# Rows of softmax sums stored from GpSimd's queue and gates stored from ScalarE's queue, both formerly from SyncE's, in a two-layer encoder

## The chip, the cores and the metric

The kernel runs on one core of a Trainium2 chip. The metric is the device time of one execution in microseconds (us), taken as the median of several runs. The engines are named as the profile names them: PE is TensorE (matmuls), DVE is VectorE, ACT is ScalarE, POOL is GpSimd, SP is SyncE, which here does nothing but issue DMAs. An issue of a DMA from ACT or SP stands in the profile as ACTq or SPq.

## The reference

A trunk of two encoder layers runs over two groups of tokens, 512 ("sample") and 256 ("prompt"), width 1024. Each layer normalises its input, modulates it by a condition, projects it, and feeds three mixers: A, dense latent attention with 8 heads; B, dilated windows with 3 x 4 heads, combined by their softmax denominators; C, 2-D neighbourhood attention with 8 heads. Each mixer is gated, projected, merged by sigmoid gates, and put through one output projection with a residual.

```python
def encoder_layer(...):
    h = rmsnorm(x, g_pre) * (1 + scale) + shift
    z = h @ w_in
    o_a = mla_attention(...)            # softmax over all tokens
    o_b = dilated_attention(...)        # softmax over three windows together
    o_c = neighbourhood_attention(...)  # softmax over 8 x 16 neighbours
    p_a = (o_a * silu(gate_a)) @ w_pa   # p_b and p_c likewise
    mg = sigmoid(merge)                 # three gates of width 1024
    out = (mg[0] * p_a + mg[1] * p_b + mg[2] * p_c) @ w_out
    return x + gate * rmsnorm(out, g_post)
```

## The kernel before, in words

Features lie on the 128 partitions and the 768 tokens of both groups side by side, 0 to 511 the sample's and 512 to 767 the prompt's. Every fp32 operand of a matmul is split into a high and a low part: ACT casts the high part, DVE or POOL subtracts (`sub_lo`, line 160), and PE runs three products. Weights come through a ring of three raw buffers (`load_split`, line 165), are split by ACT at line 177 and by `sub_lo`, and are multiplied in `feat_mm` (line 201).

For each layer the stages are `branch_a`, `branch_b`, `branch_c`, `merge`, `project`. In A and C the scores go key by key: keys on the partitions, queries along the row. A softmax (`soft_keys`, line 658) so needs a maximum and a sum across partitions. DVE first combines the key tiles (lines 662 and 664), POOL then reduces across the partitions (line 665) and leaves the result on all of them. The steps are: maximum, subtraction on DVE (line 670), exponential on ACT (line 671), sum. The exponentials are split again and multiplied with the values in `pv` (ACT line 679, DVE line 680, PE line 683; the result is o_ps); they are not divided by the sum there. Instead one row of each sum is sent to a DRAM table, `den_scr` (line 672; in B line 869). Once a pair of heads is complete, `row_gains` (line 686) reads its sums back in another shape (line 689), takes reciprocals on DVE (line 690), writes those (line 691) and reads them spread over the partitions (line 695). DVE multiplies the pair's outputs with them (line 655; in C line 1012), and `finish_pair` sends them to DRAM (line 446) for `merge`, which loads them again (line 1046).

The small tiles of a softmax (the combined maximum, the reduced maximum, the combined sum, the reduced sum) are slots of a ring of six, `S`. The stored row lies in such a slot, so the slot is free only when the store has read it.

To keep PE busy during the softmaxes, `early` (line 1021) multiplies gates of the merge stage ahead of time. ACT writes tanh of such a gate into a tile `the` (line 1019; one buffer), and a DMA takes it to `th_scr` in DRAM (line 1027). The table `FILL` says how many gates go where. In `merge` the gates come back (line 1051).

POOL runs reductions, some of the low parts (every second or third, by the table `LO_POOL`), additions and memsets. Between reductions and plain tensor operations the program has an operation without operands (`ISA` in the order of instructions), by which POOL changes from one kind to the other.

A scheduler sets the order of instructions on each engine. It follows the dependences and its own model of durations, and the engine that issues a DMA is part of what it plans with; an edit of one issue can so move instructions everywhere. Each engine, and each engine's DMA issues, runs in order: what stands behind a waiting instruction waits with it.

The lines that the change touches are 672, 869 and 1027. Lines named below have the same numbers in both kernels.

Of the kernel before, what the change touches and what calls it, by code (L numbers as in the profile page):

```python
# [16 lines left out]
ALU = mybir.AluOpType  # L17
# [49 lines left out]
def trunk_kernel(ctx, tc, x_t, c_row, c_col, w_ada0, w_ada, cols, w_a, w_feat, w_val, w_val2, w_uqk, w_qr, w_uv, w_pj, w_o,  # L67
                 bias_s, bias_p, rope_t, rope_k, mask_b, mask_c, y_t):
    nc = tc.nc
# [18 lines left out]
    def U(tag, dt=F32, name=None):  # L88
        return pool.tile([P, T], dt, tag=tag, name=name or tag, bufs=BUFS[tag])
# [51 lines left out]
    th_scr = dram.tile([depth, 24, P, T], F32, name="th_scr")  # L141
    row_scr = dram.tile([depth, 28, P], F32, name="row_scr")
    den_scr = dram.tile([depth, 10, 2, 1, T], F32, name="den_scr")
# [241 lines left out]
    def halves(t):  # L385
        return t[:, :256], t[:, 256:]
# [92 lines left out]
    def latents(l, h, hl):  # L479
# [87 lines left out]
        while pend:  # L567
            flip(*pend.pop(0))
        early(l, h, min(LATE_E, FILL[l][0]))
        do_jobs(gates, GATES[l][-1], c_)  # L570
        ada_gain(l)
        pend = [(j, (3, 4, 5)) for j in range(6)]
        early(l, h, FILL[l][0] - LATE_E, lambda k, mm: flips(mm))
        while pend:
            flip(*pend.pop(0))
        return cn, krs

    def branch_a(l, h_, h):
# [13 lines left out]
        va = None  # L592
        for pr in range(4):
            early(l, h, FILL[l][1 + 2 * pr])
            if pr % 2 == 0:

# [34 lines left out]
            for e in range(2):  # L631
                hd = (pr % 2) * 2 + e
                (qs, qrs), ka = qn[e], kn[e]
                prods = ((ka, qs), (kb[e], qs), (krs, qrs))
                tq = [U("tq") for _ in range(4)]
                for g, (o, n) in enumerate(GROUPS):
                    nk = n // P

                    for k0 in range(0, nk, 1 + g):
                        sp = SP()  # L640
                        for k in range(1 + g):
                            kc = slice(o + (k0 + k) * P, o + (k0 + k + 1) * P)
                            for j, (w, a) in enumerate(prods):
                                nc.tensor.matmul(sp[:, k * 256:k * 256 + n], w[:, kc], a[:, o:o + n],
                                                 start=(j == 0), stop=(j == 2))
                        for k in range(1 + g):
                            nc.scalar.copy(tq[k0 + k][:, o:o + n], sp[:, k * 256:k * 256 + n])  # L647
                for g, (o, n) in enumerate(GROUPS):
                    xs = [x[:, o:o + n] for x in tq[:n // P]]
                    soft_keys(xs, n, den_scr[l, pr, e, 0:1, o:o + n])  # L650
                    o_ps = ps_o.tile([P, NS], F32, tag="o", name="o_ps")[:, :n]
                    for k, x in enumerate(xs):
                        pv(x, [(o_ps, vslice(va, hd, o // P + k), lambda a: a)], k == 0, k == n // P - 1)
                    out_half(o_ps, o_t, e, [(lambda a: a[:, o:o + n], lambda a: a)])
# [3 lines left out]
    def soft_keys(xs, n, den):  # L658

        def across(op):  # L660
            out, red = (S(), S()) if n > 256 else halves(S())
            nc.vector.tensor_tensor(out, xs[0], xs[1], op=op)  # L662
            for x in xs[2:]:
                nc.vector.tensor_tensor(out, out, x, op=op)
            nc.gpsimd.partition_all_reduce(red, out, P, RED.max if op == ALU.max else RED.add)  # L665
            return red

        m = across(ALU.max)
        for x in xs:
            nc.vector.tensor_sub(x, x, m)  # L670
            nc.scalar.activation(x, x, AF.Exp)  # L671
        nc.sync.dma_start(out=den, in_=across(ALU.add)[0:1])

    def pv(x, terms, first, last):

# [112 lines left out]
    def branch_b(l, h, hl):  # L788
# [4 lines left out]
        for hd in range(4):  # L793
            e = hd % 2
# [38 lines left out]
            for g, (o, n) in enumerate(GROUPS):  # L833
# [32 lines left out]
                across(sm, ALU.add)  # L866
                dn = S()
                nc.gpsimd.partition_all_reduce(dn[:, :n], sm[:, :n], P, RED.add)  # L868
                nc.sync.dma_start(out=den_scr[l, 4 + hd // 2, e, 0:1, o:o + n], in_=dn[0:1, :n])

                o_ps = ps_o.tile([P, NS], F32, tag="o", name="o_ps")
                ov = o_ps[:, :n].rearrange("p (s i) -> p s i", s=SB[g])
# [75 lines left out]
    def branch_c(l, h, hl):  # L948
        state["phase"] = "c"
        vcs = None  # L950
        for pr in range(4):
# [12 lines left out]
            for e in range(2):  # L964
# [30 lines left out]
                for g, (o, n) in enumerate(GROUPS):  # L995
                    xs = [x[:, o:o + n] for x in tq]
                    soft_keys(xs, n, den_scr[l, 6 + pr, e, 0:1, o:o + n])
                    o_ps = ps_o.tile([P, NS], F32, tag="o", name="o_ps")
                    v = lambda k: vslice(vc, hd % 4, k)
                    if g == 0:  # L1000
                        lo_, hi_, mid = (lambda a: a[:, 0:256]), (lambda a: a[:, 256:512]), (lambda a: a[:, 128:384])
                        pv(xs[0], [(c(o_ps), v(k), c) for k, c in ((0, lo_), (2, hi_))], True, False)
                        pv(xs[1], [(c(o_ps), v(k), c) for k, c in ((1, mid), (3, ends))], False, True)
                    else:
                        for k in range(2):
                            pv(xs[k], [(o_ps[:, :256], v(4 + k), lambda a: a)], k == 0, k == 1)
                    out_half(o_ps, o_t, e, natural(g))
# [8 lines left out]
    def merge_gate(l, idx, h, th, between=None):  # L1016
        mg = feat_mm(w_feat[l, F_MG + idx], KT, h, name="mg", between=between)
        for g, (o_, n) in enumerate(GROUPS):
            nc.scalar.activation(th[:, o_:o_ + n], mg[g], AF.Tanh, scale=0.5)  # L1019

    def early(l, h, n, between=None):

        for _ in range(n):
            idx = 23 - len(ahead)
            th = U("f", name="the")
            merge_gate(l, idx, h, th, between)
            nc.sync.dma_start(out=th_scr[l, idx], in_=th)
            ahead.add(idx)

    def do_jobs(jobs, n, cact):  # L1030
# [170 lines left out]
    for t_ in range(T // P):  # L1201
        x, x2 = U("cv", name="x"), x2s[t_ // 3][:, t_ % 3 * 256:t_ % 3 * 256 + 256]
        nc.sync.dma_start(out=x, in_=x_t[t_, :, :T])
        if t_ % 3 == 0:
            nc.sync.dma_start(out=x2s[t_ // 3].rearrange("p (t c) -> p t c", c=256),
                              in_=x_t[t_:t_ + 3, :, T:].rearrange("t p c -> p t c"))
# [22 lines left out]
    for t_, pieces in enumerate(xs):  # L1229
        for i, x in enumerate(pieces):  # L1230
            e = (NORM0, NORM1)[i][t_]
# [6 lines left out]
    for l in range(depth):  # L1238
        hl = act_list(h)
        ahead.clear()  # L1240
        branch_a(l, h, hl)
        branch_b(l, h, hl)
        branch_c(l, h, hl)
        mixed = merge(l, hl)
        h = project(l, mixed, l == depth - 1)
# [166 lines left out]
```

## Time and profile before

| what | us |
|---|---|
| median of 3 runs | 1964.03 (1962.99 to 1964.36) |
| the profiled execution | 1966.35 |
| its span, from the first instruction to the last | 1964.6 |
| PE busy | 1845.0 (94%) |
| DVE busy | 1530.9 (78%) |
| ACT busy | 1018.6 (52%) |
| POOL busy | 664.2 (34%) |

The time of the profiled execution is that of one run, 2.3 us above the median; the span is what the trace covers. Busy times overlap between engines. A busy PE isn't PE at its peak, since matmuls are pipelined and the clock that is granted to PE varies between two levels, 1.2 and 2.4 GHz; the profile gives it as a share of the higher one for any stretch.

### The profile page before, as it was taken

What the parts mean: (1) busy time and instruction counts of PE and PEld (TensorE: products, weight loads), DVE (VectorE), ACT (ScalarE), POOL (GpSimd) and SP (SyncE); (2) the same over time, 40 slices, a digit from 0 to 9 for tenths busy, and PEclk for the clock granted to TensorE, in tenths of its full rate; (3) what the DMA queues carried; (4) which work ended last, traced back from release to release, by engine and by line L of the source; (5) the groups of instructions that cost most, each with busy time, mean ns of one, the idle gap of its engine ahead of it and who ended that gap; (6) DMA issues with size and microseconds to landing.
All of it is one profiled execution on the core that took longest, in us unless ns stands there. A gap on an engine that the chain in (4) does not pass through costs nothing. (4 is left out here: it accounts for less than half of the span.)

```text
span 1964.6 us, 30204 instructions
## 1 busy us (share of the span) xinstructions
PE 1845.0 (94%) x10674; PEld 1638.1 (83%) x10674; DVE 1530.9 (78%) x3018; ACT 1018.6 (52%) x2123; POOL 664.2 (34%) x432
## 2 busy tenths in 40 slices
PE   7897999999989987999999999999999999987998
PEld 6886888888877876888999888889888778876898
DVE  8957768579987999896587467687699868997763
ACT  5356556356577455322464356574566684653241
POOL 6404415202221454316534024253022212454570
PEclk9998999999999999999999999999999999998999
DMA  8432241232313233445452332422222222233652
GB/s 294 150 117 62 86 139 57 71 99 82 92 54 92 79 117 115 167 143 191 140 197 89 124 99 88 135 76 86 87 85 85 88 75 89 87 107 99 217 174 71
DMA packets 94904, 221.25 MB, mean 113 GB/s; under 512 B 18096, under 2 KB 32504, under 8 KB 94752
## 3 DMA queue, kind: packets, MB, share of 16 engines
q1 hardware_dynamic: 90144, 213.02, 33.4%
q10 hardware_dynamic: 4608, 6.29, 1.1%
q8 instruction: 84, 1.38, 0.3%
q14 instruction: 68, 0.56, 0.1%
HBM read 173.78 MB, written 28.18 MB: 103 GB/s over the span
## 5 line engine op out<-in xcount | busy, mean ns | idle before, releaser
L665 POOL PARTITION_ALL_REDUCE fixed<-fixed x128 | 314.2, 2486 | 496.3 <-DVE fixed L662 337.0
L201 PE MATMUL mg<-fixed 128*128 128x512 f32 (+1 forms) x2304 | 436.2, 342 | 1.4 <-DVE o_t L397 0.7
L201 PEld LDWEIGHTS mg<-fixed 128*128 128x128 f32 x2304 | 360.3, 191 | 51.6 <-PE sp L984 1.0
L177 ACT CAST fixed<-fixed 128x512 fp32r<-128x512 f32 (+1 forms) x332 | 199.5, 606 | 339.3 <-PE mg L201 117.8
L160 DVE TENSOR_TENSOR fixed<-fixed,fixed 128x512 fp32r<-128x512 f32 (+3 forms) x309 | 224.2, 729 | 113.9 <-ACT fixed L177 110.7
L201 PE MATMUL qkb<-fixed 128*128 128x512 f32 (+1 forms) x1152 | 211.9, 338 | 0.0
L201 PEld LDWEIGHTS qkb<-fixed 128*128 128x128 f32 x1152 | 177.0, 189 | 24.2
L201 PE MATMUL gate<-fixed 128*128 128x512 f32 (+1 forms) x960 | 184.0, 341 | 1.6 <-DVE tq L830 1.3
L201 PEld LDWEIGHTS gate<-fixed 128*128 128x128 f32 x960 | 150.0, 191 | 22.0 <-DVE tq L830 1.5
L1064 PE MATMUL pp<-hi,fixed 128*128 128x512 f32 (+1 forms) x640 | 161.5, 340 | 5.0 <-ACT th L1019 4.7
L680 DVE TENSOR_TENSOR fixed<-tq,fixed 128x512 fp32r<-128x512 f32 (+1 forms) x160 | 127.9, 821 | 2.7 <-ACT fixed L679 2.5
L1064 PEld LDWEIGHTS pp<-hi,fixed 128*128 128x128 f32 x640 | 111.9, 192 | 19.9 <-ACT th L1019 5.1
L671 ACT ACTIVATE tq<-tq 128x512 f32<-128x512 f32 (+1 forms) x160 | 83.4, 545 | 82.7 <-DVE tq L670 82.5
L429 POOL MEMSET kb<- 64x768 f32 x56 | 41.1, 736 | 209.5 <-PE sp L820 121.0
L670 DVE TENSOR_TENSOR tq<-tq,fixed 128x512 f32<-128x512 f32 (+1 forms) x160 | 97.8, 660 | 16.3 <-POOL fixed L665 16.2
L1163 PE MATMUL op<-wo,fixed 128*128 128x384 f32 (+1 forms) x648 | 108.2, 320 | 1.8 <-POOL wo L160 1.8
L1064 PE MATMUL pp<-lo,fixed 128*128 128x512 f32 (+1 forms) x320 | 108.9, 341 | 0.8 <-DVE lo L160 0.8
L1163 PEld LDWEIGHTS op<-wo,fixed 128*128 128x128 f32 x648 | 101.3, 188 | 3.2 <-POOL wo L160 3.1
L311 DVE SCALAR_TENSOR_TENSOR fixed<-tm,fixed 128x768 f32<-128x768 f32 (+1 forms) x128 | 93.3, 729 | 2.1 <-DMA tm<-in_w_ada_dram 0.4
L868 POOL PARTITION_ALL_REDUCE fixed<-fixed x16 | 49.0, 3084 | 128.4 <-DVE fixed L845 65.7
L662 DVE TENSOR_TENSOR fixed<-tq 128x256 f32<-128x256 f32 (+1 forms) x128 | 79.1, 623 | 14.3 <-ACT tq L647 10.8
L679 ACT CAST fixed<-tq 128x512 fp32r<-128x512 f32 (+1 forms) x160 | 80.8, 530 | 11.0 <-PE o_ps L683 8.2
(245 smaller groups left out, 3910.7 us busy)
## 6 DMA issues: line engine op xcount, KB each, us to landing
fixed<-in_w_feat_dram SPq DMA_DIRECT2D x108, 512.0 KB
th_scr<-the SPq DMA_DIRECT2D x35, 384.0 KB
th<-th_scr SPq DMA_DIRECT2D x35, 384.0 KB
tm<-in_w_ada_dram SPq DMA_DIRECT2D x32, 384.0 KB
fixed<-in_w_val_dram SPq DMA_DIRECT2D x20, 512.0 KB
xs<-xb SPq DMA_DIRECT2D x96, 96.0 KB
fixed<-in_w_pj_dram SPq DMA_DIRECT2D x32, 256.0 KB
fixed<-in_w_o_dram SPq DMA_DIRECT2D x16, 512.0 KB
```

Of the source, the lines that this page charges most:

```text
L160: eng.tensor_sub(out, a, b)
L177: nc.scalar.copy(hi[:, :m], raw[:, o:o + m])
L201: state["mm"] = nc.tensor.matmul(outs[g], w[:, wsl], a[g], start=(i == 0 and wi == 0), stop=(i == nk - 1 and wi == 2))
L311: nc.vector.scalar_tensor_tensor(junk, x, 1.0, c, ALU.mult, ALU.mult, accum_out=ada2[:, l, i, g, j:j + 1])
L662: nc.vector.tensor_tensor(out, xs[0], xs[1], op=op)
L665: nc.gpsimd.partition_all_reduce(red, out, P, RED.max if op == ALU.max else RED.add)
L670: nc.vector.tensor_sub(x, x, m)
L671: nc.scalar.activation(x, x, AF.Exp)
L679: nc.scalar.copy(hi, x)
L680: nc.vector.tensor_sub(lo, x, f(hi))
L1064: nc.tensor.matmul(pp, w[:, ws], o[k][a][:, o_:o_ + n], start=(i == 0), stop=(i == 3 * nk - 1))
L1163: mm = nc.tensor.matmul(op[cc], m[a][g][:, k, c0:c0 + P], parts[k][cc][b], start=(k == 0 and i == 0), stop=(k == KT - 1 and i == 2))
```

## The change

The stores of softmax sums (80 in all: 64 at line 672, 16 at line 869) are issued by POOL, and the stores of gates ahead (35 at line 1027) by ACT. SP issued both before. What is stored, and where, stays.

```diff
 def soft_keys(xs, n, den):
...
-        nc.sync.dma_start(out=den, in_=across(ALU.add)[0:1])
+        nc.gpsimd.dma_start(out=den, in_=across(ALU.add)[0:1])
...
 def branch_b(l, h, hl):
...
                 nc.gpsimd.partition_all_reduce(dn[:, :n], sm[:, :n], P, RED.add)
-                nc.sync.dma_start(out=den_scr[l, 4 + hd // 2, e, 0:1, o:o + n], in_=dn[0:1, :n])
+                nc.gpsimd.dma_start(out=den_scr[l, 4 + hd // 2, e, 0:1, o:o + n], in_=dn[0:1, :n])
...
 def early(l, h, n, between=None):
...
             merge_gate(l, idx, h, th, between)
-            nc.sync.dma_start(out=th_scr[l, idx], in_=th)
+            nc.scalar.dma_start(out=th_scr[l, idx], in_=th)
```

The order of instructions changes with it. On SP, in layer 0's dense branch, during the first two pairs of heads, before:

```order
L1027 DMA th_scr<-the 128x768
L165 DMA fixed_73<-in_w_feat_dram 128x1024 x2
L672 DMA den_scr<-fixed_73 1x256
L672 DMA den_scr<-fixed_73 1x512
L623 DMA qrs<-qrh 32x768 x4
L623 DMA qrs<-qrl 32x768 x4
L672 DMA den_scr<-fixed_73 1x256
L165 DMA fixed_73<-in_w_feat_dram 128x1024
L672 DMA den_scr<-fixed_73 1x512
L165 DMA fixed_73<-in_w_uv_dram 128x512
L689 DMA fixed_73<-den_scr 128x12
```

And the same place on SP in the changed kernel:

```order
L165 DMA fixed_73<-in_w_feat_dram 128x1024 x2
L623 DMA qrs<-qrh 32x768 x4
L623 DMA qrs<-qrl 32x768 x4
L165 DMA fixed_73<-in_w_feat_dram 128x1024
L165 DMA fixed_73<-in_w_uv_dram 128x512
L689 DMA fixed_73<-den_scr 128x12
```

The five stores are gone, and the loads, the copies of rotary queries (line 623) and the read of the sums follow each other in the order that they had.

In branch C of layer 0, second pair of heads, on PE: `qc` are query projections for the third pair, `sp` (lines 984 and 988) the scores of the second head, `o_ps` the first head's product with the values. Before:

```order
L683 MATMUL o_ps<-fixed_72,vb 128x256 x5
L201 MATMUL qc_6521<-fixed_72 128x512
L201 MATMUL qc_6522<-fixed_72 128x256
L201 MATMUL qc_6521<-fixed_72 128x512
L201 MATMUL qc_6522<-fixed_72 128x256
L201 MATMUL qc_6521<-fixed_72 128x512
L201 MATMUL qc_6522<-fixed_72 128x256
L201 MATMUL qc_6521<-fixed_72 128x512
L984 MATMUL sp<-qs,ka 128x256
L984 MATMUL sp<-qs,kb 128x256
L984 MATMUL sp<-qs,ka 128x2x128
L984 MATMUL sp<-qs,kb 128x2x128
```

And in the changed kernel:

```order
L988 MATMUL sp<-qs,kb 128x256
L988 MATMUL sp<-qs,ka 128x256
L988 MATMUL sp<-qs,kb 128x256
L201 MATMUL qc_6522<-fixed_72 128x256
L201 MATMUL qc_6521<-fixed_72 128x512
L201 MATMUL qc_6522<-fixed_72 128x256
L201 MATMUL qc_6521<-fixed_72 128x512
L201 MATMUL qc_6522<-fixed_72 128x256
L201 MATMUL qc_6521<-fixed_72 128x512
L201 MATMUL qc_6522<-fixed_72 128x256
L201 MATMUL qc_6521<-fixed_72 128x512
L683 MATMUL o_ps<-fixed_72,vb 128x256
```

The second head's scores stood behind the first head's first six o_ps matmuls; they now stand ahead of the first of them.

At the end of branch C of layer 1, on POOL: the reductions of the last two pairs (line 665), and among them one low part of the merge stage (line 160, `lo<-ox`) with a change of kind on either side. Before:

```order
L429 MEMSET kb 64x768 x2
L665 ISA fixed_73<-fixed_73 128x256
L665 ISA fixed_73<-fixed_73 128x512
L665 ISA fixed_73<-fixed_73 128x256
L160 ISA
L160 TENSOR_TENSOR lo<-ox,hi 128x768
L665 ISA
L665 ISA fixed_73<-fixed_73 128x512
L665 ISA fixed_73<-fixed_73 128x256
L665 ISA fixed_73<-fixed_73 128x512 x2
```

And in the changed kernel:

```order
L672 DMA den_scr<-fixed_73 16x1x16
L665 ISA fixed_73<-fixed_73 128x512
L665 ISA fixed_73<-fixed_73 128x256
L672 DMA den_scr<-fixed_73 16x1x32
L665 ISA fixed_73<-fixed_73 128x512
L160 ISA
L160 TENSOR_TENSOR lo<-ox,hi 128x768
L665 ISA
L665 ISA fixed_73<-fixed_73 128x256
L665 ISA fixed_73<-fixed_73 128x512
L672 DMA den_scr<-fixed_73 16x1x16
L665 ISA fixed_73<-fixed_73 128x512
```

Three reductions stand between the last memsets and the change of kind in both, but two of them are now 512 wide and one 256, where it was one and two. The stores stand among the reductions, some of them one reduction later than the sum that they send.

At the same place on PE, where `mg` are the last gates, o_ps the last pair's products with the values and `pp` the merge stage's projection. Before:

```order
L201 MATMUL mg_17247<-fixed_72 128x256
L201 MATMUL mg_17246<-fixed_72 128x512
L201 MATMUL mg_17247<-fixed_72 128x256
L201 MATMUL mg_17246<-fixed_72 128x512
L201 MATMUL mg_17247<-fixed_72 128x256
L683 MATMUL o_ps<-fixed_72,vb 128x256 x5
L683 MATMUL o_ps<-fixed_72,vb 128x2x128 x2
L683 MATMUL o_ps<-fixed_72,vb 128x256 x4
L1064 MATMUL pp<-hi,fixed_72 128x512
L1064 MATMUL pp<-lo,fixed_72 128x512
```

And in the changed kernel:

```order
L201 MATMUL mg_17247<-fixed_72 128x256
L683 MATMUL o_ps<-fixed_72,vb 128x256 x4
L1064 MATMUL pp<-hi,fixed_72 128x512
L1064 MATMUL pp<-lo,fixed_72 128x512
L1064 MATMUL pp<-hi,fixed_72 128x512 x2
L1064 MATMUL pp<-lo,fixed_72 128x512
L1064 MATMUL pp<-hi,fixed_72 128x512 x2
L1064 MATMUL pp<-lo,fixed_72 128x512
L1064 MATMUL pp<-hi,fixed_72 128x512 x2
L1064 MATMUL pp<-lo,fixed_72 128x512
L1064 MATMUL pp<-hi,fixed_72 128x512
L683 MATMUL o_ps<-fixed_72,vb 128x256
```

In both kernels one more o_ps matmul of this head stands earlier, among the gates: behind 37 of that gate's 48 matmuls before, behind 46 now. The eleven others came in one piece; now four come, then twelve of the projection's, then the other seven.

## Rows read from the trace of the kernel before

**Rows 1.** The page's head and its part 1: busy us (share) x instructions.

```profile
span 1964.6 us, 30204 instructions
PE 1845.0 (94%) x10674; PEld 1638.1 (83%) x10674; DVE 1530.9 (78%) x3018; ACT 1018.6 (52%) x2123; POOL 664.2 (34%) x432
```

**Rows 2.** Stretches of 50 us: busy us of PE, PEld, DVE, ACT, POOL; clock; DMA.

```profile
700.00:750.00 50.00, 41.29 (x235) 35.32 (x234) 48.66 (x88) 29.88 (x62) 26.01 (x12) 0.95 0.39 127
...
1650.00:1700.00 50.00, 50.00 (x303) 44.15 (x302) 49.28 (x93) 25.36 (x55) 22.62 (x14) 1.00 0.25 83
...
1750.00:1800.00 50.00, 38.10 (x194) 32.22 (x194) 37.05 (x62) 23.22 (x46) 16.68 (x8) 0.82 0.27 84
```

**Rows 3.** Waits of SP's queue: who waited for whom, us in total, times, longest.

```profile
SPq L165 <- DVE fixed L160: 351.2, 91, 31.9
SPq L672 <- POOL fixed L665: 143.2, 34, 10.0
SPq L1027 <- ACT the L1019: 106.5, 23, 11.1
...
SPq L869 <- POOL fixed L868: 43.0, 12, 9.6
```

**Rows 4.** Waits of POOL.

```profile
POOL fixed L665 <- DMA den_scr<-fixed: 16.0, 4, 6.9
```

**Rows 5.** Waits of DVE.

```profile
DVE o_t L655 <- DMA den<-rden_scr: 25.8, 7, 5.1
...
DVE tq L670 <- POOL fixed L665: 16.2, 7, 10.4
...
DVE tq L855 <- POOL fixed L853: 3.4, 2, 1.7
```

**Rows 6.** DMA issues by tile: ns min/median/max, first and last start in us.

```profile
L672 SPq DMA_DIRECT2D den_scr<-fixed x64: 215/239/287, 165.1 to 1819.8; - x64
```

```profile
L1027 SPq DMA_DIRECT2D th_scr<-the x35: 319/327/530, 111.0 to 1728.3; - x35
```

```profile
L973 ACTq DMA_DIRECT2D fixed<-in_bias_p_dram x16: 334/334/361, 602.6 to 1790.2; - x16
```

**Rows 7.** POOL by line: busy us, mean ns | idle before, with releasers.

```profile
L665 POOL PARTITION_ALL_REDUCE fixed<-fixed x128 | 314.2, 2486 | 496.3 <-DVE fixed L662 337.0 <-DVE fixed L664 98.3 <-PE kn L201 26.4
...
L429 POOL MEMSET kb<- 64x768 f32 x56 | 41.1, 736 | 209.5 <-PE sp L820 121.0 <-DMA th_scr<-the 21.8 <-DMA den<-rden_scr 14.2
```

**Rows 8.** Timeline of POOL, end of branch C in layer 1: start, us, what, idle before.

```profile
1770.72 1.80 POOL L665 PARTITION_ALL_REDUCE fixed<-fixed  x1 [10.19 <-DVE fixed L662]
1780.53 1.84 POOL L160 TENSOR_TENSOR lo<-ox,hi 128x768 fp32r<-128x768 f32 x1 [8.02 <-DVE fixed L690]
1788.33 2.87 POOL L665 PARTITION_ALL_REDUCE fixed<-fixed  x2 [5.96 <-issue]
1794.46 9.23 POOL L665 PARTITION_ALL_REDUCE fixed<-fixed  x3 [3.26 <-DVE fixed L662]
```

**Rows 9.** Timeline of PE at the same place.

```profile
1780.28 6.75 PE L201 MATMUL mg<-fixed 128*128 128x512 f32 x37
1793.12 0.58 PE L683 MATMUL o_ps<-fixed,vb 128*128 128x256 f32 x1 [6.08 <-ACT fixed L679]
1793.50 3.62 PE L201 MATMUL mg<-fixed 128*128 128x256 f32 x11
...
1804.14 0.63 PE L1064 MATMUL pp<-hi,fixed 128*128 128x512 f32 x1
```

**Rows 10.** Timelines of DVE and of ACT at the same place.

```profile
1790.16 1.73 DVE L670 TENSOR_TENSOR tq<-tq,fixed 128x512 f32<-128x512 f32 x2 [10.42 <-POOL fixed L665]
```

```profile
1794.64 0.70 ACT L679 CAST fixed<-tq 128x256 fp32r<-128x256 f32 x2
```

**Rows 11.** Timeline of DVE, one pair of heads earlier.

```profile
1737.82 2.73 DVE L680 TENSOR_TENSOR fixed<-tq,fixed 128x512 fp32r<-128x512 f32 x1
...
1743.43 0.68 DVE L680 TENSOR_TENSOR fixed<-tq,fixed 128x512 fp32r<-128x512 f32 x1
```

## The prediction, made before the changed kernel was run

> **What bounds the kernel now.** First the page's head: of a span of 1964.6 us TensorE (PE) is busy 1845.0, VectorE (DVE) 1530.9, ScalarE (ACT) 1018.6, GpSimd (POOL) 664.2 [rows 1]. So PE sets the time; only what shortens or lengthens its 1964.6 - 1845.0 = 119.6 us of idle, or the time that it runs at the lower clock, can change it. Then the stretches of 50 us [rows 2]: the idle isn't spread evenly. In 1650 to 1700 PE is never idle, though DVE is busy 49.28 us of 50; in 700 to 750 it idles 8.7 us and in 1750 to 1800 11.9 us, with a granted clock of 0.95 and 0.82. Both are the end of the neighbourhood branch, where the softmaxes run out of gate matmuls to hide behind. Then what SyncE's queue (SP) waited for [rows 3]: 143.2 + 43.0 us at the stores of softmax sums, for POOL's reductions, and 106.5 us at the stores of the gates, for ACT's tanh. That is 292.7 us in which a queue in order held back the loads behind it, but the largest entry is another one, 351.2 us at weight loads that wait for the buffer to be split. Last, who suffers: POOL waited 16.0 us, four times, for a store of sums to release a ring slot [rows 4]; DVE waited 25.8 us for the spread reciprocals, and 16.2 + 3.4 us, in 7 + 2 waits, for a maximum from POOL [rows 5]. None of PE's own waits in its list ended with a transfer.
>
> **The change, part by part.** It has no arithmetic in it: each edit moves an issue. All times below are set against the one profiled execution, 1966.35 us with a span of 1964.6; that is 2.3 us above the median of the three runs, 1964.03, and my time is for the median.
>
> *Taken from SP.* 80 stores of sums at 0.24 us and 35 of gates at 0.33 us [rows 6] are 80 x 0.24 + 35 x 0.33 = 31 us of issuing, and the 292.7 us of waits. SP computes nothing and is on PE's path only through what arrives late, and the weight loads' own wait stays. I book nothing for it; if that is wrong, the second rival says what it gives.
>
> *Given to ACT.* 35 stores. ACT's own DMA issues now take 0.33 us [rows 6]: 35 x 0.33 = 12 us on an engine that is idle 946 us. Each store comes behind the tanh that writes its tile, on the same engine, so it waits for little. Bounds: 0 to 12 us; I take 0, since PE has its three PSUM buffers per group in front of ACT there. If that cover were gone (two gates in a row, with ACT late), the next eviction would be 0.33 us late.
>
> *Given to POOL.* 80 stores on an engine that is idle 1300 us. The trace has no DMA issued by POOL, so its price is bounded: below by an issue on SP, 0.24 us, above by POOL's software reduction, 2.49 us [rows 6, 7]. I take 0.74 us, the memset [rows 7], since it is the row of POOL nearest in kind: it reads no tensor, as a store's issue computes nothing. That is 59 us of POOL (19 to 199). What it costs is told by what stands behind it: POOL is in order, and a maximum behind a store starts that much later. The 128 reductions of the dense and neighbourhood branches start after 496.3 us of idle, 3.9 us each [rows 7], so most stores fall into idle time; the cover is gone where DVE already waits for POOL, which it did 9 times [rows 5]. That is 9 x 0.74 = 6.7 us for DVE. PE sees a fifth of it, as it idles 17% and 24% of the two worst stretches [rows 2] and has other matmuls in the rest: **+1.3 us** (0 to 9 x 2.49 = 22).
>
> *The order.* The scheduler places everything anew. In the dense branch the excerpt of SP's queue shows the stores gone and the loads in almost their old order. What I can price is the end of layer 1's neighbourhood branch. Before, POOL's sequence there is: a reduction at 1770.72, then a switch to a plain tensor operation (line 160, at 1780.53 after 8.02 us of idle), then back to reductions at 1788.33, after 5.96 us with nothing to wait for [rows 8]. The first maximum of the last head pair stands behind both. DVE waits 10.42 us for it [rows 10], and PE, which began its last 37 gate matmuls at 1780.28, runs dry for 6.08 us before the first o_ps matmul of that head at 1793.12 and reaches the projection's matmuls at 1804.14 [rows 9]. In the new order one more reduction 512 wide stands ahead of the switch. By counting the sums (each has its store behind it) it is this maximum; what falls behind the switch instead is a sum of the head before, which PE doesn't need. On PE 46 gate matmuls, not 37, stand ahead of the first o_ps matmul, and twelve of the projection's among the twelve o_ps. My working: 48 gate matmuls from 1780.28 at 6.75 / 37 = 0.18 us end at about 1789; the first group's eight o_ps and twelve projection matmuls at about 0.21 us follow without a wait, to 1793. The prompt's maximum, which the last four o_ps need, now comes fourth behind the switch, not second. The first two took 2.87 us together [rows 8], so four take 5.7, and two stores 1.5: 1788.33 + 7.2 = 1795.6. From such a maximum (ended at 1788.33 + 2.87 = 1791.2) to the copies on ACT (1794.64 + 0.70) were 4.1 us [rows 8, 10]; two subtractions on DVE add 2 x 0.68 [rows 11], four matmuls 0.4: 1801.5. The old order had all this, the twelve projection matmuls included, done at 1804.14 + 12 x 0.21 = 1806.7: a gain of 5.2. If DVE stretches the reductions as it did the three from 1794.46 (9.23 us, 3.1 each), four take 12.3, 6.6 more, and it is a loss of 1.4. Both were seen within 20 us; about the middle, **-2.0 us**. At the dearer store it is 2 x 1.75 = 3.5 worse, a loss of 4.9 at most. Should PE keep the higher clock where its eleven gate matmuls took 3.62 us, 0.33 each for 0.18, it is 1.6 better, a gain of 6.8 at most.
>
> *Sum.* -2.0 + 1.3 = -0.7 us: 1965.65 against the profiled execution, **1963.3 us** against the median. A measurement of this kernel can tell about 0.2%, 3.9 us, from no change, so the forecast is no change: the tail gains a little, the stores' price eats most of that, and the large number, SP's 292.7 us, was off the path. Chance 0.38. Its own range is 1960.1 to 1967.9.
>
> **The rivals.** *Faster by the new order of the softmax stages, 0.24.* PE idles 8.7 + 11.9 = 20.6 us in the two stretches named [rows 2]. In the new order the scores of a pair's second head stand ahead of its first head's o_ps matmuls, which they followed before, so the second chain through DVE, POOL and ACT begins earlier. Were half the idle saved, it is 1964.0 - 10.3 - 0.7 = 1953. For it: PE's order differs just there. Against: DVE is busy 49.28 of 50 us in 1650 to 1700, and a chain that starts earlier only queues there.
>
> *Faster by SP, 0.12.* Loads that no longer stand behind a store arrive earlier, and the 16.0 + 25.8 = 41.8 us that POOL and DVE lost to transfers [rows 4, 5] shrink. If a fifth of that reaches PE, 8.4 us: 1964.0 - 8.4 - 0.7 = 1955. For it: the stores' waits are frequent. Against: PE has no wait that ended with a transfer, and a reciprocal needs the store of sums anyway, whoever issues it.
>
> *Slower: the store's price on POOL, 0.26.* A store stands in front of the next maximum, and DVE, then ACT, then PE wait for it. Here the whole price passes through at the 9 places where DVE already waits for POOL, and the tail's gain shrinks by two stores. With a price p that is 9p - 2.0 + 2 x (p - 0.74), over 3.9 from p = 0.67 us on; with only the fifth that I took it would be from 1.95 us. At 1.6 us, midway from the memset to the reduction, it is 14.4 - 2.0 + 1.7 = 14.1: 1978. At 2.49 us it would be 22.4 - 2.0 + 3.5 = 23.9: 1988. What would make it dear is there to see: DVE and POOL hold each other up, the same subtraction at line 680 taking 2.73 us beside a reduction and 0.68 without one [rows 11]. Against: 3.9 us of idle ahead of a reduction. The Trainium skill ("SBUF — State Buffer", the section on SBUF's two separate sides) says of this very move that a DMA from GpSimd has its descriptors written by GpSimd's cores, which are shut out while VectorE runs an operation in a two-port mode, and it advises the queues of ScalarE or SyncE instead; no row here shows it, as POOL issues no DMA. By that rule the stores would come late behind such operations, which points to this rival. The skill's page "DMA: Bandwidth & Descriptors" (section Specifications) gives about 1 us to the first byte on that path; an estimate with that price gives a fifth of 9 x 1.0 = 1.8 for the stores and 1.5 of gain for the tail, 1964.3.
>
> **How the numbers follow.** No change 0.38, faster 0.24 + 0.12 = 0.36, slower 0.26: together 1. The range 1948 to 1979 reaches past 1953 and 1955 by about half of what they gain, and takes in the slower case up to 1.6 us a store; left out are stores at 2.49 us (1988) and an order that saves all 20.6 us of idle, no more than 2 in 10 together. The bounds of ACT (12 us) and of the tail (-6.8 to +4.9) lie inside it.
>
> **What would show it.** POOL gets 80 issues; if they last about 0.7 us and DVE's wait for POOL at lines 670 and 855 stays near 20 us, the price is right; at 30 us or more the third rival has it. At the end of layer 1 PE's idle of 6.08 us before o_ps should shrink or vanish and a shorter one come before the second group. SP's waits at lines 672, 869 and 1027 are gone and those of line 165 grow, with PE's idle near 118 us: then SP was off the path. PE's idle under 110 us with the two stretches better filled speaks for the first rival, and DVE's 25.8 us falling by half with it for the second. A forecast of no change is wrong if the clock's share differs: if the mean granted clock of the whole run moves by 0.005 or more, the new order decided and not the queues.

## The result, and the profile after

The changed kernel takes 1975.83 us (median of 4 runs, 1974.82 to 1977.24), the kernel before 1964.19 us in the same series (4 runs, 1962.99 to 1965.1): 11.6 us slower, a ratio of 1.006 with a 95% interval of 1.0043 to 1.0078. I had forecast no change. The profiled execution took 1975.0 us, its span is 1973.2, so the two traces lie 8.6 us apart, less than the medians. The page's head and part 1 of the changed kernel, to be laid beside [rows 1]:

```profile
span 1973.2 us, 30159 instructions
...
PE 1841.9 (93%) x10674; PEld 1637.8 (83%) x10674; DVE 1543.2 (78%) x3018; ACT 1020.0 (52%) x2123; POOL 684.2 (35%) x512
```

POOL has its 80 issues (432 instructions became 512) and is 20 us busier; the issues themselves take 40 us, but its reductions at line 665 took 301.3 us where they had taken 314.2. PE is not busier; its idle has grown from 119.6 to 1973.2 - 1841.9 = 131.3 us. Where, the stretches tell; the first three answer to [rows 2]. The changed kernel:

```profile
700.00:750.00 50.00, 39.63 (x229) 34.41 (x227) 48.70 (x86) 27.08 (x57) 23.20 (x17) 0.92 0.41 131
1650.00:1700.00 50.00, 50.00 (x304) 44.39 (x303) 49.25 (x90) 26.05 (x55) 23.22 (x17) 1.00 0.25 83
1750.00:1800.00 50.00, 38.36 (x218) 32.68 (x217) 36.72 (x63) 24.11 (x44) 19.12 (x14) 0.93 0.29 90
1800.00:1850.00 50.00, 35.76 (x205) 31.96 (x206) 33.87 (x57) 16.62 (x34) 13.42 (x11) 0.83 0.38 120
1750.00:1850.00 100.00, 74.12 (x423) 64.64 (x423) 70.60 (x119) 40.73 (x78) 32.54 (x24) 0.88 0.33 105
```

And the last two of these in the kernel before:

```profile
1800.00:1850.00 50.00, 47.96 (x266) 41.61 (x267) 41.33 (x68) 17.46 (x34) 19.13 (x11) 0.94 0.58 181
1750.00:1850.00 100.00, 86.06 (x459) 73.83 (x459) 78.38 (x129) 40.68 (x80) 35.81 (x18) 0.88 0.42 132
```

Between 1750 and 1850 us PE idles 25.9 us where it idled 13.9. These 12.0 us are all that its idle grew by in the whole span (11.7), and they lie behind 1800, at the end of layer 1's branch C: from 1750 to 1800 the idle is 11.6 us, against 11.9 before. The granted clock over the 100 us is 0.88 in both, so the loss there is idle time and not clock.

The queues did what the change says. SP's waits, as in [rows 3], after the change:

```profile
SPq L165 <- DVE fixed L160: 612.9, 105, 32.5
...
SPq L689 <- DMA den_scr<-fixed: 55.9, 14, 13.4
```

The waits at lines 672, 869 and 1027 are gone, and SP waits longer for weight buffers instead, 612.9 us for 351.2. That is what a queue off the path looks like. One other wait has grown: at line 689, the read of the sums, SP waited 55.9 us for their stores, where it was 23.5. A store's price on POOL (line 672, ns min/median/max, first and last start), and DVE's waits, as in [rows 5]:

```profile
L672 POOL DMA_DIRECT2D den_scr<-fixed x64: 484/500/832, 165.3 to 1822.8; - x64
```

```profile
DVE o_t L655 <- DMA den<-rden_scr: 20.8, 6, 5.1
DVE fixed L690 <- DMA fixed<-den_scr: 19.2, 7, 4.4
...
DVE o_t L1012 <- DMA den<-rden_scr: 11.3, 5, 5.4
...
DVE fixed L662 <- POOL fixed L665: 9.4, 1, 9.4
...
DVE tq L670 <- POOL fixed L665: 6.7, 7, 2.2
...
DVE tq L855 <- POOL fixed L853: 3.4, 2, 1.7
```

A store takes 0.50 us. DVE's wait for a maximum at line 670 has fallen from 16.2 to 6.7 us: the reductions don't come late in general. But one combine (line 662) now waits 9.4 us for POOL.

The other waits of DVE changed less: at line 655 20.8 us for 25.8, at line 690 19.2 for 17.6, at line 1012 11.3 for 5.4.

The timelines of the tail show how that wait became the loss (start, us, what, idle before). POOL, in the changed kernel:

```profile
1783.34 2.14 POOL L160 TENSOR_TENSOR lo<-ox,hi 128x768 fp32r<-128x768 f32 x1 [8.01 <-DVE o_t L397]
1791.35 5.05 POOL L665 PARTITION_ALL_REDUCE fixed<-fixed  x2 [5.87 <-issue]
1796.27 0.71 POOL L672 DMA_DIRECT2D den_scr<-fixed  x1
...
1799.19 1.03 POOL L665 PARTITION_ALL_REDUCE fixed<-fixed  x1
```

DVE:

```profile
1793.19 2.49 DVE L662 TENSOR_TENSOR fixed<-tq 128x256 f32<-128x256 f32 x1 [9.42 <-POOL fixed L665]
...
1799.90 0.23 DVE L690 RECIPROCAL fixed<-fixed 128x12 f32<-128x12 f32 x1 [3.02 <-DMA fixed<-den_scr]
...
1805.81 1.57 DVE L1012 TENSOR_TENSOR o_t<-o_t,den 128x448 f32<-128x448 f32 x3 [2.52 <-DMA den<-rden_scr]
...
1807.90 0.75 DVE L670 TENSOR_TENSOR tq<-tq,fixed 128x256 f32<-128x256 f32 x2
```

PE:

```profile
1778.31 8.29 PE L201 MATMUL mg<-fixed 128*128 128x512 f32 x46
...
1796.34 1.01 PE L683 MATMUL o_ps<-fixed,vb 128*128 128x256 f32 x3 [6.06 <-DVE fixed L680]
1814.24 1.22 PE L683 MATMUL o_ps<-fixed,vb 128*128 128x256 f32 x4 [16.89 <-ACT th L1019]
...
1815.47 0.41 PE L1064 MATMUL pp<-lo,fixed 128*128 128x256 f32 x1
```

The last of these, the prompt's first projection matmul with a low part, stands at the same place in PE's order in both kernels; in the kernel before:

```profile
1807.92 0.28 PE L1064 MATMUL pp<-lo,fixed 128*128 128x256 f32 x1
```

Read together: PE begins its last gate 2.0 us earlier than in [rows 9]. By then 75 of the 80 stores of sums and all 35 of the gates have been issued, so in these two traces they had cost PE nothing up to there. On POOL the change of kind (the two idles of 8.01 and 5.87 us) now stands ahead of a sum: that of the third pair's second head, for the prompt. DVE's combine for the next maximum waits 9.42 us for the first reduction behind it (presumably for that one's slot of the ring); the low part of line 680 stands behind it, and PE idles 6.06 us. Then the late sum is stored, read back, and DVE stands at its reciprocal (3.02 us) and at the multiplication with it (2.52 us). Behind these, in order, stands the prompt's subtraction for the last pair's first head. Its maximum was reduced at 1800.2; it starts at 1807.9. So PE idles another 16.89 us before the last four o_ps matmuls of that head. (The page puts this down to a tanh on ACT; ACT itself was waiting for DVE's line 680 before that.)

### The profile page after: what moved, and what is told of

Same layout as the page of the kernel before. It is cut to its first block, busy times and chain, and to the rows that moved or that the text cites. A ratio compares the mean times of both kernels' runs of the same rounds, so it can differ in the third digit from the quotient of the medians.

```text
span 1973.2 us, 30159 instructions
## 1 busy us (share of the span) xinstructions
PE 1841.9 (93%) x10674; PEld 1637.8 (83%) x10674; DVE 1543.2 (78%) x3018; ACT 1020.0 (52%) x2123; POOL 684.2 (35%) x512
## 4 chain that ended last, share of the span: by engine, by line
PE 51%; DVE 27%; issue 7%; ACT 7%; POOL 4%; DMA 4%; SPq 1%; DVEq 0%; ACTq 0%; POOLq 0%
PE mg L201 14%; PE op L1163 6%; PE pp L1064 4%; PE qkb L201 4%; PE gate L201 4%; PE vp L753 3%; DVE fixed L160 3%; DVE fixed L680 3%; DVE tq L670 2%; POOL fixed L665 2%; PE cq L554 2%; PE qc L201 2%; PE sp L644 2%; PE kc L201 2%; ACT hc L923 2%
## 5 line engine op out<-in xcount | busy, mean ns | idle before, releaser
L665 POOL PARTITION_ALL_REDUCE fixed<-fixed x128 | 301.3, 2382 | 480.0 <-DVE fixed L662 314.9
L201 PE MATMUL mg<-fixed 128*128 128x256 f32 (+1 forms) x2304 | 436.4, 341 | 4.9 <-DVE u L440 3.8
L160 DVE TENSOR_TENSOR fixed<-fixed,fixed 128x512 fp32r<-128x512 f32 (+3 forms) x309 | 230.8, 750 | 99.2 <-ACT fixed L177 95.9
L680 DVE TENSOR_TENSOR fixed<-tq,fixed 128x512 fp32r<-128x512 f32 (+1 forms) x160 | 136.1, 870 | 3.1 <-ACT fixed L679 2.8
L868 POOL PARTITION_ALL_REDUCE fixed<-fixed x16 | 45.6, 2866 | 128.1 <-issue 50.0
L679 ACT CAST fixed<-tq 128x512 fp32r<-128x512 f32 (+1 forms) x160 | 81.2, 531 | 11.4 <-PE o_ps L683 11.3
```

The source lines that it names most:

```text
L160: eng.tensor_sub(out, a, b)
L201: state["mm"] = nc.tensor.matmul(outs[g], w[:, wsl], a[g], start=(i == 0 and wi == 0), stop=(i == nk - 1 and wi == 2))
L679: nc.scalar.copy(hi, x)
L680: nc.vector.tensor_sub(lo, x, f(hi))
```

## The experiments

Theory T says just that: the order of the tail, through DVE's queue. Theory P says that 80 stores on POOL have a price wherever they stand. Theory A is the same for the 35 stores on ACT. Each ratio is to runs of the kernel before in the same series.

### 1 and 2: one half of the change at a time

Experiment 1 keeps the edits at lines 672 and 869 alone, experiment 2 the one at line 1027.

> Theory T (tail order): the loss of 11.6 us arises at the end of layer 1's branch C, where a sum of the head before now stands behind POOL's change of kind and holds up DVE's queue. Only the 80 stores of sums go to POOL here, the gates' stores stay on SP, and POOL and DVE have there the order of the changed kernel: 1973 to 1978, with a PE idle of some 17 us before the last o_ps matmuls. Theory P (price): 80 stores on POOL cost what they last and more, wherever they stand: 1973 to 1978 as well. Theory A (ACT): the loss comes from the 35 stores of gates on ACT: 1962 to 1966.

> Only the 35 stores of gates go to ACT; the sums stay on SP, and POOL has at the end of layer 1 the order of before, with the changes of kind ahead of the last pair's first maximum. Theory T: 1961 to 1967, no idle of PE above 10 us there. Theory P: 1961 to 1967. Theory A: 1972 to 1978.

Measured: sums only 1977.41 us, 1.0058 (1.0046 to 1.0070); gates only 1968.38 us, 1.0017 (1.0007 to 1.0026). The stores of sums make the loss, with the same order in the tail (a PE idle of 17.3 us before the last four o_ps). The gates alone came out just above the 1961 to 1967 of T and P and below the 1972 to 1978 of A: their part is small, but not nothing, and A falls as the main cause.

### 3 and 6: no change of kind, with the stores moved and not

In both layers the low parts of branch B's two tiles in the merge stage are made by DVE; POOL had made one of them in each layer. Layer 0's stood behind the softmaxes already (in the kernel before at 865.4 us, the last reduction at 792.2), so the change of kind that goes from among reductions is layer 1's.

```diff
-                o.append(split_to("st", x))
+                state["lo"] += b == 1
+                o.append(split_to("st", x, nc.vector if b == 1 else None))
```

> The changed kernel with the low parts of the two dilated branch tiles in the merge stage on DVE, so that POOL has no change of kind among the last softmaxes of either layer. All 80 stores stay on POOL, and 35 on ACT. Theory T: the two idles of POOL (8.0 and 5.9 us) and with them most of the 10.6 us that the tail lost go: 1958 to 1967, PE idle before the last o_ps matmuls under 8 us. Theory P: the stores are all there, so 1972 to 1977. Theory A: 1972 to 1977.

> The control to the third experiment: the kernel before, all its stores on SP, with the same low parts on DVE, so no change of kind among the last softmaxes. Theory T: before loses less there (one PE idle of 6.1 us), so 1957 to 1963; against the third experiment the difference is what 80 + 35 stores on other queues cost or give without the tail: within 4 us either way. Rival R (the stores relieve SP and that, not the missing change of kind, made the third experiment fast): this kernel stays at 1963 to 1968.

Measured: all stores moved, 1958.54 us, 0.9969 (0.9958 to 0.9979); no store moved, 1954.42 us, 0.9930 (0.9915 to 0.9946). The tail in experiment 3:

```profile
1750.00:1850.00 100.00, 90.39 (x508) 78.83 (x509) 80.09 (x141) 44.75 (x86) 46.73 (x32) 0.97 0.49 159
```

And in experiment 6:

```profile
1750.00:1850.00 100.00, 91.89 (x501) 78.28 (x500) 84.00 (x138) 40.27 (x78) 47.13 (x24) 0.95 0.50 156
```

PE's idle there is 9.6 and 8.1 us, where it was 25.9 with the stores moved and 13.9 before. With the change of kind in place the moved stores cost 0.60%, without it 0.39%. So taking out the change of kind gives the changed kernel 0.91% and the kernel before 0.70%, and a remainder of 0.39%, 7.7 us, has nothing to do with it. The two stand in different series, and with both intervals that is some 0.2 to 0.6% (the medians themselves are 4.1 us apart); T had allowed 4 us. Each of the two kernels keeps its base's order but for rows round those low parts and in the tail behind them.

### 4: all stores moved but the last eight

`soft_keys` is given the engine of its store; branch C passes SP for the last two pairs of layer 1, everything else stays as in the changed kernel.

```diff
-def soft_keys(xs, n, den):
+def soft_keys(xs, n, den, q=None):
...
-        nc.gpsimd.dma_start(out=den, in_=across(ALU.add)[0:1])
+        (q or nc.sync).dma_start(out=den, in_=across(ALU.add)[0:1])
```

> The changed kernel with only the 8 stores of layer 1's last two pairs of branch C back on SP. 72 of 80 stores stay on POOL and all 35 on ACT; in that tail the maximum of the last pair's first head stands ahead of POOL's change of kind and the two sums of the head before have no order of the changed kernel. Theory T: 1956 to 1966. Theory P: nine tenths of the loss stay, 1973 to 1976. Theory A: 1973 to 1977.

Measured: 1960.29 us, 0.9975 (0.9965 to 0.9986). With 107 of 115 stores moved the kernel is faster than before. The order that came of it has the change of kind two reductions later.

### 16: only the last eight moved

> The kernel before with only the 8 stores of layer 1's last two pairs on POOL, and the change of kind left where it is: on POOL the last pair's first maximum comes behind it, as before, not a sum of the head before. Theory T (it is this order that costs): 1960 to 1968, a ratio of 0.997 to 1.002. If 8 stores there make the loss whatever the order: 1.004 to 1.007.

Measured: 1966.84 us, 0.9998 (0.9989 to 1.0007). Eight stores on POOL in the critical place, with the order of before around the change of kind, cost nothing.

### 5: the reciprocal held back

In the changed kernel layer 1's third pair is closed only behind the last low part (line 680) of the fourth pair's first head.

```diff
+            for pr_, o_t_, u_ in held:
+                with ExitStack() as es:
+                    if l and pr_ == 2:
+                        es.enter_context(tc.issue_after(state["sub30"].ins))
+                    den = row_gains(l, 6 + pr_)
...
```

> The changed kernel, with the reciprocal, the multiplication and the store of layer 1's third pair told to come behind the last subtraction (line 680) of the fourth pair's first head on each engine. POOL's order, its change of kind included, stays word for word; DVE's, PE's and ACT's differ only in this tail. Theory T in its full form (DVE in order: the reciprocal that waits for the late sum holds up the next head): of the two waits of DVE, 3.0 + 2.5 us, and the 1.8 us of work between them most leaves the path: 4 to 8 us less than the changed kernel, a ratio to before of 1.0015 to 1.0040. Rival S (the change of kind alone, by POOL's 8.0 + 5.9 us of idle and DVE's wait of 9.4 us for it): within 2 us of the changed kernel, a ratio of 1.005 to 1.007.

Measured: 1968.77 us, 1.0006 (0.9997 to 1.0016), more than I expected. DVE in experiment 5:

```profile
1792.50 2.49 DVE L662 TENSOR_TENSOR fixed<-tq 128x256 f32<-128x256 f32 x1 [7.60 <-POOL fixed L665]
...
1802.12 0.76 DVE L670 TENSOR_TENSOR tq<-tq,fixed 128x256 f32<-128x256 f32 x2
...
1807.66 0.22 DVE L690 RECIPROCAL fixed<-fixed 128x12 f32<-128x12 f32 x1
```

POOL's order is unchanged and the wait for it is still 7.60 us, but the subtraction now starts at 1802.12, not at 1807.90, and the reciprocal comes after it and waits for nothing. Rival S falls: what cost most was not POOL's idle itself but what stood in DVE's queue because of it.

### 17 and 18: the place of the change of kind

Both tell layer 1's splits of branch B's two tiles in the merge stage, and with the low part that POOL makes the change of kind, which reduction they have to follow: in experiment 17 (the changed kernel) the late sum, in 18 (the kernel before) the first maximum of the last pair.

```diff
+                with ExitStack() as es:
+                    if l and b == 1:
+                        es.enter_context(tc.issue_after(state["hold"].ins))
+                    o.append(split_to("st", x))
```

> The changed kernel, all 115 stores moved, with one order given: in layer 1 the low part of the merge stage on POOL, and so the change of kind, comes behind the 256 sum of the third pair's second head, which in the changed kernel stands behind it. Theory T: the late reciprocal and DVE's wait of 9.4 us for that sum go; 8 to 16 us less than the changed kernel, a ratio to before of 0.9975 to 1.0020. Price theory: the stores are all there, 1.0040 to 1.0070.

> The kernel before, all stores on SP, with the change of kind told to come behind the first maximum of layer 1's last pair; the sum of the head before stays ahead of it too. This is the order that I took the changed kernel to have. Theory T: the maximum ahead is worth what the prediction gave it or more, 2 to 8 us: 0.9955 to 0.9990. If any order other than that of before costs there, or if what stands behind the change of kind does not matter, 1.000 to 1.006.

Measured: 17 1966.90 us, 1.0008 (0.9999 to 1.0018); 18 1960.19 us, 0.9978 (0.9967 to 0.9989). DVE in experiment 17, where the edit adds two lines (the subtraction is line 672, the reciprocal 692):

```profile
1791.35 0.23 DVE L692 RECIPROCAL fixed<-fixed 128x12 f32<-128x12 f32 x1 [2.39 <-DMA fixed<-den_scr]
1798.98 1.60 DVE L672 TENSOR_TENSOR tq<-tq,fixed 128x256 f32<-128x256 f32 x2 [7.39 <-POOL fixed L665]
```

All 115 stores are moved, and the order is the changed kernel's up to this tail: on POOL the sum's reduction stands ahead of the change of kind, and two stores and another reduction shift by a place. With that 0.52% of 0.60% are gone: the reciprocal runs 8.5 us earlier, the subtraction 8.9. Experiment 18, which differs from the kernel before in the tail alone, has the order that I took the changed kernel to have, and it is faster than before by 4.3 us, more than the 2.0 that I had priced it at.

### 7 and 14: stores issued twice

Without the change of kind, the 64 stores of line 672 are issued a second time, to a table that nobody reads: by POOL on top of experiment 3, by SP on top of experiment 6.

```diff
-        nc.gpsimd.dma_start(out=den, in_=across(ALU.add)[0:1])
+        red = across(ALU.add)[0:1]
+        nc.gpsimd.dma_start(out=den2, in_=red)
+        nc.gpsimd.dma_start(out=den, in_=red)
```

> The third experiment's kernel, with each of the 64 stores at line 672 issued a second time by POOL, to a table that nobody reads: 64 x 0.5 = 32 us more on POOL. Theory T (the price of a store is small and lies in POOL's idle time): within 4 us of the third experiment, 1956 to 1963. Theory P (a store's price is passed on): 8 to 32 us more, 1967 to 1991.

> The sixth experiment's kernel with the 64 stores of line 672 issued twice by SP: the control for the seventh. If doubling is paid on POOL's queue, this one stays within 3 us of the sixth: 0.9915 to 0.9945. If it is the traffic, or only that the program is ordered anew, it loses what the seventh lost, 7 to 8 us: 0.9960 to 0.9975.

Measured: 7 1969.63 us, 1.0012 (1.0000 to 1.0023); 14 1957.38 us, 0.9950 (0.9938 to 0.9962). Against their own bases that is +0.43% on POOL, 8.4 us for 64 x 0.50 = 32 us of issues, and +0.20% on SP. T's "under 4 us" was wrong. About a quarter of the price came through (by the medians 11.1 us, a third), though half as much as that comes from SP too. Both kernels are ordered anew throughout, so neither figure is a price alone.

### 8, 12, 13, 15: where the remainder sits

All without the change of kind, from experiment 6: 8 moves the sums alone, 12 the gates alone, 13 the last eight sums alone, 15 all sums but these.

> The third experiment's kernel with the gates' stores back on SP. Theory T: the tail's order is that of the third experiment, so 1955 to 1961. If the 35 stores on ACT cost what the second experiment was slower by (0.17%, with its own order), 1953 to 1957; if they help by relieving SP, 1960 to 1964.

> The sixth experiment's kernel with only the 35 gates' stores on ACT; with the third, sixth and eighth it makes the four combinations of the two moves without the change of kind. If the stores on ACT cost what the second experiment was slower by (0.17%), 0.9940 to 0.9955; if that was the order of its tail, within 2 us of the sixth: 0.9920 to 0.9940.

> The sixth experiment's kernel (no change of kind, 0.9930 to before) with only the 8 stores of layer 1's last two pairs of branch C on POOL; everything ahead keeps the sixth's order. Place theory (the remainder arises in the last two pairs): 4 to 8 us above the sixth, a ratio of 0.9950 to 0.9975. Price theory (0.1 us a store, wherever it is): under 1 us above the sixth, 0.9920 to 0.9940.

> The complement: the sixth experiment's kernel with 72 sums on POOL and the last 8 on SP, the gates' stores on SP. Place theory: within 2 us of the sixth, 0.9920 to 0.9940. Price theory: nine tenths of what the eighth lost, 0.9950 to 0.9965.

| moved | median, us | ratio | interval |
|---|---|---|---|
| nothing (6) | 1954.42 | 0.9930 | 0.9915 to 0.9946 |
| last 8 sums (13) | 1951.45 | 0.9921 | 0.9908 to 0.9934 |
| 72 sums (15) | 1961.94 | 0.9973 | 0.9960 to 0.9986 |
| 80 sums (8) | 1959.75 | 0.9955 | 0.9939 to 0.9970 |
| 35 gates (12) | 1958.80 | 0.9966 | 0.9955 to 0.9977 |
| all 115 (3) | 1958.54 | 0.9969 | 0.9958 to 0.9979 |

The place theory falls: the last two pairs cost nothing, the 72 sums elsewhere 0.43%. Gates alone cost 0.36%, sums alone 0.25%, both 0.39%, where prices per store would add up to 0.61%. That hints at orders and not prices but doesn't show it: the six runs stand in four series, and each difference is uncertain by some 0.2%. Experiment 13 has the lowest time of all.

### 9 to 11: the hold without the change of kind

The hold of experiment 5, for the third pair of both layers, on top of experiments 3, 6 and 7.

> The third experiment's kernel (all stores moved, no change of kind) with the third pair's reciprocal, multiplication and store of both layers held behind the last subtraction (line 680) of the fourth pair's first head. It was 0.4% slower than the sixth experiment's kernel, which has the stores on SP. Theory T: that remainder is the same thing in small, DVE standing at a late reciprocal or multiplication ahead of the next head (2.1 us in layer 0, then a PE idle of 7.4 us), so the hold takes 3 to 7 us off the third experiment: a ratio to before of 0.9930 to 0.9955. Theory P (the remainder is the price of 80 stores on POOL and 35 on ACT): within 2 us of the third experiment, 0.9960 to 0.9980.

> The control: the sixth experiment's kernel (stores on SP, no change of kind) with the same hold. DVE hardly waited for a reciprocal there, so theory T expects it within 2 us of the sixth experiment, a ratio of 0.9920 to 0.9940, and the ninth within 3 us of it. If the hold is good whatever the stores do, it gains here as much as in the ninth: 0.9900 to 0.9915.

> The seventh experiment's kernel (64 stores issued twice) with the hold. Doubling had cost 0.43%, against what I expected. Theory T: a second store delays the sum's round trip and is paid by DVE at the reciprocal, so with the hold doubling costs under 3 us against the ninth. Theory P: it is paid by the reductions behind it, whatever DVE's order: 6 to 10 us above the ninth.

Measured: 9 1959.57 us, 0.9971 (0.9958 to 0.9984); 10 1955.66 us, 0.9950 (0.9938 to 0.9962); 11 1965.90 us, 1.0006 (0.9997 to 1.0014). The hold takes nothing off experiment 3, so the remainder is not the late reciprocal of the third pair; T falls there, and 9 lies where theory P had it. Doubling still costs 0.35%, 6.3 us, again as P expected. Experiment 10, which moves no store and adds no work, is 0.20% above experiment 6, but their intervals overlap. That a new order alone is worth that much shows in experiment 18, 0.22% below the kernel before with the stores and the work unchanged.

## Why the prediction was wrong

*What bounds the kernel, and SP at nothing:* right. SP lost 292.7 us of waits [rows 3] and PE gained nothing. The waits that the second rival built on did shrink, from 41.8 us to 8.8 + 20.8 = 29.6, and nothing of it reached PE.

*POOL's 80 stores, +1.3 us:* the price was 0.50 us, not 0.74, and DVE's waits for a maximum, which I took to carry it, fell from 16.2 to 6.7 us at line 670 and stayed at 3.4 at line 855. So the third rival's mechanism is not what happened, and that the measured 1975.83 us lies inside the range of 1948 to 1979 is luck: its upper end was set by stores at 1.6 us each. That stores on POOL are nearly free is right for the last eight (experiments 13 and 16). For the other 72 it is open: 0.25 to 0.43% without the change of kind, 5 to 8 us, where an order alone is worth 0.22% (experiment 18).

*ACT's 35 stores, 0:* too low, but inside its bounds of 0 to 12 us. Alone they cost 0.17% in experiment 2 and 0.36% in 12, price and order together.

*The end of layer 1's branch C, -2.0 us:* this is the step that failed. I wrote that what falls behind the switch "instead is a sum of the head before, which PE doesn't need". The reading of the order was right: the maximum had moved ahead and the sum behind. PE needs no such sum, but DVE does, at the reciprocal, and DVE runs in order. I had the last four o_ps matmuls and what follows done at 1801.5; they ended at about 1815.5. The prompt's maximum was ready at 1800.2, not 1795.6 (4.6 us: the change of kind ended 3 us later than I took it from [rows 8]); DVE came to its subtraction 7.7 us after that; the way from there took 7.6 us, not 5.9. Of the first group's eight o_ps matmuls, which I had run without a wait, three stood until 1796.34 for a low part behind the waiting combine. From the start of the last gate to the prompt's projection matmul shown above it is 1815.47 - 1778.31 = 37.2 us, against 1807.92 - 1780.28 = 27.6 in the old order (my 1806.7 for nearly the same place was 1 us early). In place of a gain of 2.0 us the tail lost 9.5, twice the 4.9 that I had as its worst; with the start 2.0 us earlier that leaves 7.5 of the 8.6 by which the span grew. Experiment 18 shows the half that I priced (a maximum ahead gains 0.22%), 17 and 5 the half that I left out (the sum behind costs 0.5%).

*The first rival:* PE was busy 39.63 us in 700 to 750, against 41.29, and 38.36 in 1750 to 1800, against 38.10: the stretches were not filled.

*What would show it:* the clock. The mean of the profiled run went from 0.978 to 0.974, under the 0.005 that I had set, and yet the new order decided: the sign was no use. PE's idle was to stay near 118 us and came to 131.3; the 6.08 us before the first o_ps did vanish, and the one before the second group wasn't shorter but 16.89. In 1800 to 1850, where PE idles 14.2 us, it was granted 0.83, against 0.94 before with 2.0 us of idle: where PE idled more, its clock was lower too.

**Shown:** PE's lost time is in the tail; the stores of sums make it, through the order that they lead to; moving one reduction, or holding one pair's reciprocal and what follows from it, brings the time back to within 0.1% of before with every store moved. **Open:** whether these two orders undo the loss or, like experiment 18's, are better than that of before and hide a remainder. Without a change of kind 0.39% of the 0.60% is left, and how much of that is the price of a store on POOL and how much the order of all else can't be told, since no run moves all stores and keeps the order. A third candidate stands untested, the sum's longer way: in experiment 3 SP waited 59.3 us at line 689 for the stores, in 6 23.7, and DVE 17.0 us at line 1012 for the spread reciprocals, in 6 8.5; the hold of experiment 9 covers the third pair alone.

## What to carry to other kernels

Where a scheduler orders the work, an edit of a DMA's engine is an edit of the order, and the order is what to price: at each wait that bounds the kernel, list what now stands behind it on every in-order engine, not only on the bounding one. A result that the bounding engine never reads is still on its path when another engine waits for it ahead of work that the bounding engine does need. And a switch of kind between critical reductions is worth looking for: here one low part a layer, given to another engine, gave 0.7%, while moving either queue's stores gave nothing.

## What was not expected of the hardware

The change of kind was seen before as idle of 8.02 and 5.96 us on an engine that is 34% busy [rows 8]; that taking it out of the last softmaxes gives the kernel before 0.70% (1954.42 against 1966.81 us in that series) was more than the 6.08 us of PE's idle that I had tied to it. Of the 13.4 us by which the traced span is shorter in experiment 6 (1951.2 us), 7.7 are idle of PE and 5.7 its busy time (1839.3 us), and from 1750 to 1850 the clock that it was granted is 0.95 where it was 0.88. The second idle was 5.87 to 6.31 us with nothing to wait for in the changed kernel and experiments 5, 17 and 18. The Trainium skill ("GPSIMD Engine Reference", section Instruction dispatch) gives about 6 us for the first call of a freshly loaded kernel, with no instruction in the profile; the second idle has that size, though no row shows that a load is what it is, and the first, 7.2 to 8.0 us in the same runs, is not told apart there.

Stores from POOL took 484 to 832 ns of POOL each, though DVE is 78% busy; they landed 1.5 to 5.2 us after their issue, half of them within 1.7. The rule that I weighed (the Trainium skill, "SBUF — State Buffer", section SBUF: two separate sides), by which they would be shut out while DVE runs an operation in a two-port mode, is not borne out by the issues; whether it is behind the few late landings, and which of DVE's operations here run in such a mode, no row tells.
